# S5 exponentials and first states moved from the vector engine to Pool, the direct kernels' product interleaved over two array tiles, and a higher priority for the transposed retention outputs

## The chip, the core and the metric

One core of one Trainium2 chip runs the whole program. The metric is the device time of one execution in microseconds (us), less being better; the time before is a median of three runs. The engines are PE (matrix products), DVE (vector engine), ACT (scalar engine), POOL, and SP, which here only starts DMAs.

## What is computed

One layer of a hybrid decoder on 320 rows (256 prompt positions and 8 samples of 8 positions), all in float32. A norm and one projection give the S5 input u and, for 8 heads, q, k, v and a gate g. The S5 part needs parameters of its own, worked out on the chip from 64 groups of 64 states; the retention heads run beside it.

```python
h = rms_norm(x, norm_mix);  u, q, k, v, g = split(h @ w_in)
dt = exp(log_step);  lam_bar = exp(lam * dt)              # complex: exp(re) and cos, sin
b_bar = ((lam_bar - 1) / lam) * b
x_t = lam_bar * x_(t-1) + b_bar u_t;  y = Re(C x) + d * u # per group; samples start at x0
o = retention(rotary(q), rotary(k), v);  o = group_norm(o) * gn_w * silu(g)
x = x + concat(s5_out, o) @ w_out
x = x + (silu(h2 @ w_gate) * (h2 @ w_up)) @ w_ffn_out;  y = rms_norm(x)
```

## The kernel before

Nearly all of PE's work is the large products. Each weight is split into a high and a low part in a reduced format (`hi` by ACT on line 130, `lo` by DVE on line 131), and a block of 128 by 128 weights then takes three products of 320 columns (lines 141 to 143). `wload` fetches eight blocks at a time with three buffers each; `gemm` sums 16 blocks into one of two PSUM buffers ("acc").

The first 39 us are the prologue: 16 blocks of x are split (`xhi`, `xlo`, lines 266 to 273) beside the first weights (lines 858 and 859), and four projections run together (line 868). Then follow the projections of head 0, and for each head q, k, v, a gate and one u block (lines 905 to 918). PE and POOL keep the order in which the program emits instructions (`manual_schedule`, line 835). A small clock of estimated PE time (`clk`) and a heap of generators (`spawn`, `run_due`) decide where, between the products of a projection, the small work of a head or of an S5 chunk is emitted. DVE, ACT and SP get their order from a planner, by readiness and priority; `tc.high_priority(offset=...)` moves work forward. Every engine then runs its own queue in order.

The S5 parameters: `vexp` (line 341) evaluates an exponential by a polynomial on tiles of 128 by 32 elements. It is called for dt (line 365, `s5_step`) and for `rr`, the size of lam_bar (line 409). `s5_params` computes cos and sin by polynomials (ang, lines 370 to 405), has POOL build the rotations (`s5_turns`, line 462), forms `lp` and `gp` (powers of lam_bar and the input factors) and `lx0`, the first states of the samples (line 453: six operations on 128 by 256 elements). All small scratch tiles are cut from one tile `scrt` by `newscr` and `T`.

Chunk c of the S5 part (`s5_chunk`, from line 551) is due at 53.6 + 33.4 c on that clock. It forms `bl` and `cl`, transposes `bl` (`pt`), and runs two small products: `pb`, and `pk_` (lines 612 to 618), the direct kernels. The latter has 64 output rows per group u, so two groups lie side by side in the array (`tile_position=(0, 64 * u)`); all of u = 0 is emitted before u = 1. `lx0` is read in `s5_scan` (line 534).

A head's small work: `head_k` transposes k (`pst`) and forms the scores `pss`; `head_v` transposes v, forms `po`, the norm statistics (DVE, lines 720 to 723) and the reciprocal root (POOL, lines 726 to 733), normalises on ACT (`on`, line 736), transposes back (`pn`, line 747), and scales the result by the norm weight and the gate into `retp` (line 759, on DVE where the gate exists). `pst`, `pss`, `psr`, `pn`, `pt` and `pk_` share two PSUM buffers ("misc").

Of the kernel before, what the change touches and what calls it, by code (L numbers as in the profile page):

```python
# [44 lines left out]
def hybrid_kernel(ctx, tc, xT, w_in, w_in4, w_out, w_glu, w_fi, w_fo, vecs, s5p, bc, x0,  # L45
# [9 lines left out]
    def f(t):  # L55
        return t.bitcast(F32)
# [13 lines left out]
    o = 0  # L70
# [97 lines left out]
    def ts(out, a, s1, o1, s2=None, o2=None):  # L168
        if o2 is None:
            dve.tensor_scalar(out, a, s1, None, o1)  # L170
        else:
            dve.tensor_scalar(out, a, s1, s2, o1, o2)
        return out
# [159 lines left out]
    def T(shape):  # L333
        n = int(np.prod(shape[1:]))
        a = scr[0][:, scr[1]:scr[1] + n]
        scr[1] += n
        if len(shape) == 3:
            a = a.rearrange("p (a b) -> p a b", b=shape[2])
        return a

    def vexp(out, x, shape):
        xc = ts(T(shape), x, -87.0, ALU.max, 88.0, ALU.min)
        n = ts(T(shape), xc, 1.4426950408889634, MUL, MAGIC, ADD)
        n = ts(n, n, MAGIC, SUB)
        r = stt(T(shape), n, -LN2_PARTS[0], xc, MUL, ADD)
        r = stt(r, n, -LN2_PARTS[1], r, MUL, ADD)
        q = T(shape)
        ts(q, r, 1.0 / 5040, MUL, 1.0 / 720, ADD)
        for cf in (1 / 120, 1 / 24, 1 / 6, 0.5, 1.0, 1.0):
            tt(q, q, r, MUL)  # L350
            ts(q, q, cf, ADD)
        ni = T(shape).bitcast(I32)
        ts(n, n, 127.0, ADD)
        dve.tensor_copy(ni, n)
        ts(ni, ni, 23, ALU.logical_shift_left)
        tt(out, q, ni.bitcast(F32), MUL)

    sh = [P, NPAIR]
    she = [P, 3, NPAIR]
    shx = [P, NPAIR, NB]  # L360

    def s5_step():
        newscr(0)
        dt_ = T(sh)
        vexp(dt_, prm[:, 2], sh)
        return dt_

    def s5_params(dt_):

        ang = T(she)  # L370
        tt(ang[:, 0], prm[:, 1], dt_, MUL)
        ts(ang[:, 1], ang[:, 0], 8.0, MUL)
        ts(ang[:, 2], ang[:, 0], 64.0, MUL)
        nn = ts(T(she), ang, float(1 / np.pi), MUL, MAGIC, ADD)
        ts(nn, nn, MAGIC, SUB)
        for part in PI_PARTS:
            stt(ang, nn, -part, ang, MUL, ADD)
        par = ts(T(she), nn, 0.5, MUL, MAGIC, ADD)
        ts(par, par, MAGIC, SUB)
        stt(par, nn, 0.5, par, MUL, SUB)  # L380
        tt(par, par, par, MUL)
        ts(par, par, -8.0, MUL, 1.0, ADD)
        a2 = tt(T(she), ang, ang, MUL)
        ec, es = ecs[:, 0:NE], ecs[:, NE:]
        q = T(she)
        ts(q, a2, 1.0 / factorial(13), MUL, -1.0 / factorial(11), ADD)
        for kk in (9, 7, 5, 3, 1):
            tt(q, q, a2, MUL)
            ts(q, q, (1.0 if (kk // 2) % 2 == 0 else -1.0) / factorial(kk), ADD)
        tt(q, q, ang, MUL)  # L390
        tt(es[:, 0::3], q, par, MUL)
        q = T(she)
        ts(q, a2, -1.0 / factorial(14), MUL, 1.0 / factorial(12), ADD)
        for kk in (10, 8, 6, 4, 2, 0):
            tt(q, q, a2, MUL)
            ts(q, q, (1.0 if (kk // 2) % 2 == 0 else -1.0) / factorial(kk), ADD)
        tt(ec[:, 0::3], q, par, MUL)
        for l in range(2):
            n = (NE - 1 - l + 2) // 3
            c_, s_ = ec[:, l::3][:, :n], es[:, l::3][:, :n]  # L400
            u1, u2 = T([P, n, NPAIR]), T([P, n, NPAIR])
            tt(u1, c_, c_, MUL)
            tt(u2, s_, s_, MUL)
            tt(ec[:, l + 1::3][:, :n], u1, u2, SUB)
            stt(es[:, l + 1::3][:, :n], c_, 2.0, s_, MUL, MUL)
        s5_turns(ec, es)
        newscr(1)
        lr = tt(T(sh), prm[:, 0], dt_, MUL)
        vexp(rr, lr, sh)
        tt(lp[:, 0, 0], rr, ec[:, 0], MUL)  # L410
        tt(lp[:, 1, 0], rr, es[:, 0], MUL)
        den = tt(T(sh), prm[:, 0], prm[:, 0], MUL)
        d2 = tt(T(sh), prm[:, 1], prm[:, 1], MUL)
        tt(den, den, d2, ADD)
        rden = T(sh)
        dve.reciprocal(rden, den)
        nr = ts(T(sh), lp[:, 0, 0], -1.0, ADD)
        t1 = tt(T(sh), nr, prm[:, 0], MUL)
        t2 = tt(T(sh), lp[:, 1, 0], prm[:, 1], MUL)
        tt(t1, t1, t2, ADD)  # L420
        tt(ff[:, 0], t1, rden, MUL)
        t3 = tt(T(sh), lp[:, 1, 0], prm[:, 0], MUL)
        t4 = tt(T(sh), nr, prm[:, 1], MUL)
        tt(t3, t3, t4, SUB)
        tt(ff[:, 1], t3, rden, MUL)
        r2 = tt(T(sh), rr, rr, MUL)
        tt(r4, r2, r2, MUL)

        def cmul(o, a, b, shape):

            u1, u2 = T(shape), T(shape)
            tt(u1, a[0], b[0], MUL)
            tt(u2, a[1], b[1], MUL)
            tt(o[0], u1, u2, SUB)
            tt(u1, a[0], b[1], MUL)
            tt(u2, a[1], b[0], MUL)
            tt(o[1], u1, u2, ADD)

        def ri(t, i):
            return (t[:, 0, i], t[:, 1, i])  # L440

        def rep_(t, n):
            return tuple(t[:, q].unsqueeze(1).to_broadcast([P, n, NPAIR]) for q in range(2))

        cmul(ri(lp, 1), ri(lp, 0), ri(lp, 0), sh)
        cmul(ri(lp, slice(2, 4)), rep_(lp[:, :, 1], 2), ri(lp, slice(0, 2)), [P, 2, NPAIR])
        cmul(ri(gp, slice(0, 3)), rep_(ff, 3), ri(lp, slice(0, 3)), [P, 3, NPAIR])
        newscr(0)

        def b8(a):  # L450
            return a.unsqueeze(2).to_broadcast(shx)

        cmul((lx0[:, 0], lx0[:, 1]), (x0t[:, 0], x0t[:, 1]), (b8(lp[:, 0, 3]), b8(lp[:, 1, 3])), shx)
        for q in range(2):
            for d in range(2):
                o = lpc[:, :, q, 4 * d:4 * d + 4]
                act.mul(o, lp[:, q].rearrange("p e (c j) -> p c j e", j=4), -1.0 if d > q else 1.0)
                o = gpc[:, :, q, 4 * d:4 * d + 4]
                act.copy(o[:, :, :, 0], ff[:, q].rearrange("p (c j) -> p c j", j=4))
                act.copy(o[:, :, :, 1:], gp[:, q].rearrange("p e (c j) -> p c j e", j=4))  # L460
# [90 lines left out]
    def s5_chunk(c):  # L551
# [58 lines left out]
                    mm(0.04, pb[gs, u, NC * i:NC * i + NC], bst[us, i, gs], kst[us, 2 * (i % 2) + g],  # L610
                       start=True, stop=True, tile_position=(64 * u, 64 * g))
        pk_ = misc("pk_")
        for u in range(2):
            for i in range(2):
                for q in range(2):
                    mm(0.04, pk_[64 * u:64 * u + 64, 32 * i:32 * i + 32],
                       bl[:, q, i, u].rearrange("p e h -> p (e h)"), cl[:, q, 2 * u + i, 0],
                       start=q == 0, stop=q == 1, tile_position=(0, 64 * u))
# [74 lines left out]
    def head_v(h, v_, qg, rt, R):  # L693
# [55 lines left out]
                  (pn[:, NP:].rearrange("p (b t) -> p b t", t=32)[:, :, 0:NS],  # L749
                   retp[:, h, NP:].rearrange("p (b t) -> p b t", t=NS), slice(NP, N)))  # L750
        sg = R.get("sgt")
        for i_, o, sl in pairs_:
            if sg is None:
                act.mul(o, i_, v("gn", h))
            else:
                g_ = sg[:, sl]
                if sl.start:
                    g_ = g_.rearrange("p (b t) -> p b t", t=NS)
                stt(o, i_, v("gn", h), g_, MUL, MUL)
        R["gn"] = True  # L760
        if sg is not None:
            R["sg"] = True
# [84 lines left out]
    for k1 in (1, *range(2, KT + 1, 2)):  # L847
        with tc.high_priority(offset=100000), tc.manual_schedule(engines={mybir.EngineType.SP}):
            if k0 % 2 == 0:
                raw, hi, lo = (wp.tile([P, 8, P], d, name=n, tag=n, bufs=3).rearrange("p (k o) m -> p k o m", o=4)  # L850
                               for n, d in (("raw", F32), ("hi", F32R), ("lo", F32R)))
            q = slice(k0 % 2, (k1 - 1) % 2 + 1)
            sp.dma_start(xrs[k0 // 4][:, k0 % 4:(k1 - 1) % 4 + 1], xT[:, k0:k1])
            sp.dma_start(raw[:, q], w_in4[:, k0:k1])
            if k1 == 6:
                sp.dma_start(prm, s5p)
            split_x(k0, k1)
            act.copy(hi[:, q], raw[:, q])
            last_lo = dve.tensor_tensor(lo[:, q], raw[:, q], f(hi[:, q]), SUB)
        if k1 == 6:  # L860
            with tc.issue_after(last_lo.ins):
                dt_ = s5_step()
        if k1 % 2 == 0:
            accq = square_x(k1 - 2, k1)
        for k in range(k0, k1):
            for w_, x_ in ((hi, xhi), (hi, xlo), (lo, xhi)):
                for i, ps in enumerate(accs):
                    pe.matmul(ps, w_[:, k % 2, i], x_[:, k], start=k == 0 and w_ is hi and x_ is xhi,
                              stop=k == KT - 1 and w_ is lo)
            clk.now += 1.6  # L870
        k0 = k1
# [3 lines left out]
        sp.dma_start(t_, s_)  # L875
    for c in range(2):
        load_bc(c)
    s5_params(dt_)
    ytok = []
    rg = rstd_bcast(s5, accq, misc, "n1", ytok=ytok)  # L880

# [371 lines left out]
```

## Time and profile before

| | us |
|---|---|
| median of 3 runs (1460.18 to 1461.57) | 1460.41 |
| the profiled execution, as a run | 1462.15 |
| its span, first to last instruction | 1460.0 |
| PE busy in the span | 1441.0 |
| DVE busy | 862.5 |
| ACT busy | 607.2 |
| POOL busy | 44.4 |

A span row gives the busy time of each engine. PE's matmuls overlap, and the profile counts a matmul as busy to its modelled end. A row of a timeline gives the start, the duration, the engine, the line, the operation, the tiles written and read, and in brackets how long the engine stood idle before it and what released it.

### The profile page before, as it was taken

How to read it: one execution, taken by the hardware profiler on the slowest of the kernel's cores; microseconds unless marked ns; L12 is line 12 of the kernel's file. 1: busy time of each engine (PE TensorE's matmuls, PEld its weight loads, DVE VectorE, ACT ScalarE, POOL GpSimd, SP SyncE). 2: the span in 40 equal slices, each digit the busy share in tenths (PEclk: the TensorE clock that was granted, in tenths of full speed). 3: DMA queues.
4: the chain of work that ended last, by engine and by line, in shares of the span. 5: the costliest groups of instructions: out<-in, count | busy, mean ns of one | idle time of the engine just before them, and what ended most of it. 6: DMA issues, size and time to landing. Idle time of an engine off the chain costs nothing.

```text
span 1460.0 us, 26293 instructions
## 1 busy us (share of the span) xinstructions
PE 1441.0 (99%) x10654; PEld 1425.4 (98%) x10654; DVE 862.5 (59%) x1453; ACT 607.2 (42%) x973; POOL 44.4 (3%) x110
## 2 busy tenths in 40 slices
PE   8999999999999999999999999999999999999997
PEld 8989999999999999999999999999999999999996
DVE  8988787777656756665444444444444444444454
ACT  6455555554345533333333333333333333333452
POOL 2300000000000000000000000000000000000001
PEclk9999999999999999999999999999999999999999
DMA  7545554554644475655444445444445544444543
GB/s 259 169 150 164 157 163 151 157 154 144 224 146 146 153 246 191 213 206 174 146 157 145 126 147 175 152 152 146 131 142 165 168 145 150 145 133 146 154 145 111
DMA packets 84712, 235.38 MB, mean 161 GB/s; under 512 B 16368, under 2 KB 32368, under 8 KB 84592
## 3 DMA queue, kind: packets, MB, share of 16 engines
q1 hardware_dynamic: 83680, 231.58, 49.8%
q10 hardware_dynamic: 912, 2.14, 0.5%
q8 instruction: 84, 1.38, 0.4%
q14 instruction: 36, 0.29, 0.1%
HBM read 222.63 MB, written 8.95 MB: 159 GB/s over the span
## 4 chain that ended last, share of the span: by engine, by line
PE 70%; DVE 0%; ACT 0%; DVEq 0%; issue 0%
PE ps_fg L141 7%; PE ps_fo L141 7%; PE ps_fu L143 7%; PE ps_fg L143 7%; PE ps_fo L143 7%; PE ps_fu L141 7%; PE ps_fu L142 7%; PE ps_fg L142 7%; PE ps_fo L142 7%; PE ps_o L141 1%; PE ps_o L142 1%; PE ps_o L143 1%; PE ps_g L142 1%; PE ps_g L143 1%; PE ps_g L141 1%; DVE x L176 0%
## 5 line engine op out<-in xcount | busy, mean ns | idle before, releaser
L131 DVE TENSOR_TENSOR lo<-raw,hi 128x1024 fp32r<-128x1024 f32 (+1 forms) x416 | 467.0, 1123 | 380.9 <-ACT hi L130 380.4
L130 ACT CAST hi<-raw 128x1024 fp32r<-128x1024 f32 (+1 forms) x416 | 402.0, 967 | 680.7 <-PE ps_fo L142 188.1
L141 PE MATMUL ps_fg<-hhi,hi 128*128 128x320 f32 x704 | 217.6, 309 | 0.0
L141 PE MATMUL ps_fo<-ahi,hi 128*128 128x320 f32 x704 | 217.6, 309 | 0.0
L143 PE MATMUL ps_fo<-ahi,lo 128*128 128x320 f32 x704 | 217.6, 309 | 0.0
L142 PE MATMUL ps_fo<-alo,hi 128*128 128x320 f32 x704 | 217.6, 309 | 0.0
L141 PE MATMUL ps_fu<-hhi,hi 128*128 128x320 f32 x704 | 217.4, 309 | 0.0
L142 PE MATMUL ps_fu<-hlo,hi 128*128 128x320 f32 x704 | 217.4, 309 | 0.0
L143 PE MATMUL ps_fu<-hhi,lo 128*128 128x320 f32 x704 | 217.4, 309 | 0.0
L143 PE MATMUL ps_fg<-hhi,lo 128*128 128x320 f32 x704 | 217.4, 309 | 0.0
L142 PE MATMUL ps_fg<-hlo,hi 128*128 128x320 f32 x704 | 217.4, 309 | 0.0
L141 PE MATMUL ps_p<-xhi,hi 128*128 128x320 f32 x560 | 178.0, 318 | 0.6 <-DVE q__1093 L176 0.5
L143 PE MATMUL ps_p<-xhi,lo 128*128 128x320 f32 x560 | 173.6, 310 | 0.7 <-DVE lo L131 0.7
L142 PE MATMUL ps_p<-xlo,hi 128*128 128x320 f32 x560 | 173.2, 309 | 0.0
L142 PEld LDWEIGHTS ps_fg<-hlo,hi 128*128 128x128 f32 x704 | 132.4, 188 | 0.3
L141 PEld LDWEIGHTS ps_fg<-hhi,hi 128*128 128x128 f32 x704 | 132.4, 188 | 0.3
L141 PEld LDWEIGHTS ps_fu<-hhi,hi 128*128 128x128 f32 x704 | 132.4, 188 | 0.0
L143 PEld LDWEIGHTS ps_fu<-hhi,lo 128*128 128x128 f32 x704 | 132.4, 188 | 0.0
L142 PEld LDWEIGHTS ps_fu<-hlo,hi 128*128 128x128 f32 x704 | 132.4, 188 | 0.0
L143 PEld LDWEIGHTS ps_fg<-hhi,lo 128*128 128x128 f32 x704 | 132.4, 188 | 0.0
L141 PEld LDWEIGHTS ps_fo<-ahi,hi 128*128 128x128 f32 x704 | 132.1, 188 | 0.0
L142 PEld LDWEIGHTS ps_fo<-alo,hi 128*128 128x128 f32 x704 | 132.1, 188 | 0.0
(409 smaller groups left out, 1928.6 us busy)
## 6 DMA issues: line engine op xcount, KB each, us to landing
raw<-w_fi SPq DMA_DIRECT2D x176, 512.0 KB, 3.7
raw<-w_in SPq DMA_DIRECT2D x79, 512.0 KB, 4.0
raw<-w_fo SPq DMA_DIRECT2D x64, 512.0 KB, 3.5
raw<-w_out SPq DMA_DIRECT2D x32, 512.0 KB, 3.6
raw<-w_fo SPq DMA_DIRECT2D x64, 192.0 KB, 2.4
rt<-r SPq DMA_DIRECT2D x8, 512.0 KB, 5.4
raw<-w_glu SPq DMA_DIRECT2D x8, 512.0 KB, 3.5
raw<-r SPq DMA_DIRECT2D x8, 512.0 KB, 4.2
```

Of the source, the lines that this page charges most:

```text
L130: act.copy(hi[:, :m], raw[:, :m])
L131: dve.tensor_tensor(lo[:, :m], raw[:, :m], f(hi[:, :m]), SUB)
L141: pe.matmul(ps, hi, xhi[:, k], start=k == 0, stop=False)
L142: pe.matmul(ps, hi, xlo[:, k], start=False, stop=False)
L143: pe.matmul(ps, lo, xhi[:, k], start=False, stop=k == nk - 1)
```

## The change

Four edits. `vexp` runs on POOL (23 operations instead of 22, since POOL's form has no fused multiply and add of two tiles, and the shift is a multiplication) and is called for dt and for `rr` in a new `s5_exps`, which also forms `lr`; its POOL instructions are emitted in the prologue, where `s5_step` stood. `s5_params` takes dt and `rr` from there. The first states become a generator that emits its six operations on POOL at 54.6 of the emission clock. In the direct kernels' product the loops are turned, so that u changes fastest. The scaling of the transposed outputs (`pairs_`) is given the priority offset EVAC = 1500, as the other evacuations have.

```diff
     def vexp(out, x, shape):
-        xc = ts(T(shape), x, -87.0, ALU.max, 88.0, ALU.min)
...
+        xc = pts(T(shape), x, -87.0, ALU.max, 88.0, ALU.min)
+        n = pts(T(shape), xc, 1.4426950408889634, MUL, MAGIC, ADD)
+        pts(n, n, MAGIC, SUB)
+        r, q = T(shape), T(shape)
+        for part in LN2_PARTS:
+            pts(q, n, -part, MUL)
+            ptt(r, q, xc if part == LN2_PARTS[0] else r, ADD)
+        pts(q, r, 1.0 / 5040, MUL, 1.0 / 720, ADD)
         for cf in (1 / 120, 1 / 24, 1 / 6, 0.5, 1.0, 1.0):
+            ptt(q, q, r, MUL)
+            pts(q, q, cf, ADD)
...
+        pts(n, n, 127.0, ADD, float(2 ** 23), MUL)
+        pool.tensor_copy(ni, n)
+        ptt(out, q, ni.bitcast(F32), MUL)
...
-    def s5_step():
+    def s5_exps():
+
+        newscr(1)
+        dt_, lr = T(sh), T(sh)
+        vexp(dt_, prm[:, 2], sh)
+        pool.tensor_tensor(lr, prm[:, 0], dt_, MUL)
+        vexp(rr, lr, sh)
+        return dt_, scr[1]
...
-        lr = tt(T(sh), prm[:, 0], dt_, MUL)
-        vexp(rr, lr, sh)
...
-        cmul((lx0[:, 0], lx0[:, 1]), (x0t[:, 0], x0t[:, 1]), (b8(lp[:, 0, 3]), b8(lp[:, 1, 3])), shx)
+        def first_states():
+
+            yield max(0.0, T0 + 1.0 - clk.now)
+            newscr(0)
+            cmul((lx0[:, 0], lx0[:, 1]), (x0t[:, 0], x0t[:, 1]), (b8(lp[:, 0, 3]), b8(lp[:, 1, 3])), shx,
+                 pool.tensor_tensor)
+
+        spawn(first_states())
...
-        for u in range(2):
-            for i in range(2):
-                for q in range(2):
+        for i in range(2):
+            for q in range(2):
+                for u in range(2):
                     mm(0.04, pk_[64 * u:64 * u + 64, 32 * i:32 * i + 32],
...
+        with tc.high_priority(offset=EVAC):
+            for i_, o, sl in pairs_:
...
         if k1 == 6:
-            with tc.issue_after(last_lo.ins):
-                dt_ = s5_step()
+            exps = s5_exps()
```

## Rows read from the trace of the kernel before

**Rows 1.** The page's first part: busy time of each engine, share, instructions
```profile
PE 1441.0 (99%) x10654; PEld 1425.4 (98%) x10654; DVE 862.5 (59%) x1453; ACT 607.2 (42%) x973; POOL 44.4 (3%) x110
```
**Rows 2.** Stretches: length, then busy time of PE, PEld, DVE, ACT, POOL; granted clock
```profile
60.00:100.00 40.00, 36.74 (x285) 34.39 (x283) 35.37 (x102) 17.81 (x39) 12.51 (x25) 0.96 0.46 144
95.00:100.00 5.00, 5.00 (x60) 4.52 (x60) 3.12 (x7) 2.60 (x6) 0.00 (x0) 0.66 0.70 230
100.00:1440.00 1340.00, 1339.53 (x9970) 1328.82 (x9969) 766.79 (x1181) 548.94 (x861) 19.48 (x56) 1.00 0.50 159
```
**Rows 3.** Timeline of PE, 78 to 96 us: start, duration, line, operation, idle before
```profile
78.61 0.41 PE L143 MATMUL ps_p<-xhi,lo 128*128 128x320 f32 x1 [0.70 <-DVE lo L131]
...
81.64 0.31 PE L142 MATMUL ps_p<-xlo,hi 128*128 128x320 f32 x1
81.79 0.31 PE L143 MATMUL ps_p<-xhi,lo 128*128 128x320 f32 x1
82.60 0.42 PE L141 MATMUL ps_p<-xhi,hi 128*128 128x320 f32 x1 [0.50 <-DVE q__1093 L176]
...
95.00 1.38 PE L102 MATMUL pss<-q__1093,k__1169 128*128 128x256 f32 x6 [1.93 <-DVE retp L180]
```
**Rows 4.** Timeline of DVE: the two scalings of head 0's transposed outputs
```profile
87.01 0.48 DVE L180 SCALAR_TENSOR_TENSOR retp<-pn,vec,sg 128x256 f32<-128x256 f32 x1
...
94.67 0.28 DVE L180 SCALAR_TENSOR_TENSOR retp<-pn,vec,sg 128x64 f32<-128x64 f32 x1
```
**Rows 5.** Stretch of the second exponential, instructions on the scratch tile: length, DVE busy
```profile
58.90:67.80 8.90, 6.17 (x19) 1.00 0.36 121
```
**Rows 6.** Tile scrt: first four of the six operations of the first states
```profile
L176 DVE TENSOR_TENSOR scrt<-x0t,lp x4: 417/418/421, 74.2 to 79.6; 128x256 f32<-128x256 f32 x4
```
**Rows 7.** Timeline of all engines, 63 to 66 us: DVE and POOL side by side
```profile
63.15 1.72 DVE L131 TENSOR_TENSOR lo<-raw,hi 128x1024 fp32r<-128x1024 f32 x1
63.86 1.60 POOL L479 TENSOR_TENSOR e<-e,ta 128x256 f32<-128x256 f32 x1
64.79 0.71 DVE L170 TENSOR_SCALAR scrt<-scrt 128x32 f32<-128x32 f32 x1
```
**Rows 8.** Timeline of POOL: an operation on 32 elements
```profile
68.31 0.27 POOL L488 TENSOR_TENSOR tabl<-tabl,ta 128x32 f32<-128x32 f32 x1
```
**Rows 9.** Timelines of DVE and PE in the prologue: low weights formed, and first used
```profile
15.33 1.16 DVE L859 TENSOR_TENSOR lo<-raw,hi 128x1024 fp32r<-128x1024 f32 x1
...
19.04 0.31 PE L868 MATMUL py<-xhi,lo 128*128 128x320 f32 x1
```
**Rows 10.** Tile prm, the input of the exponentials: DMA issue (last: start) and landing
```profile
L856 SPq DMA_DIRECT2D prm<-s5p x1: 701/701/701, 4.6 to 4.6; - x1
...
DMA to landing us min/median/max: 6.5/6.5/6.5
```
**Rows 11.** Timelines of DVE and POOL at the start
```profile
3.42 4.73 DVE L170 TENSOR_SCALAR xhi<-u,vec 128x320 fp32r<-128x320 f32 x1 [3.42 <-DMA vec<-vecs]
...
7.74 0.24 POOL L464 MEMSET e<- 128x64 f32 x1
```
**Rows 12.** Direct kernels, chunk 1: timeline, tile view, and its matmuls in two stretches
```profile
131.13 0.91 PE L102 MATMUL pk__1760<-cl,bl 128*64 128x32 f32 x16
131.97 0.42 PE L141 MATMUL ps_p<-xhi,hi 128*128 128x320 f32 x1
...
L102 PE MATMUL pk__1760<-cl,bl x16: 222/223/243, 131.1 to 131.8; 128*64 128x32 f32 x16
...
131.12:131.38 0.26, 0.25 (x4) 1.00 0.36 125
131.38:131.58 0.20, 0.20 (x10) 1.00 0.12 26
```
**Rows 13.** Timelines of DVE and PE: the first norm's root, and its first reader
```profile
43.52 0.15 DVE L180 SCALAR_TENSOR_TENSOR ry<-rt,ry 128x3 f32<-128x3 f32 x1
...
45.81 0.49 PE L102 MATMUL ps_r<-ident,ry 128*128 128x128 f32 x3
```

More of the change, by code (lines that the diff above doesn't have):

```diff
@@ L341, in vexp, with pts @@
     def vexp(out, x, shape):
-        xc = ts(T(shape), x, -87.0, ALU.max, 88.0, ALU.min)
[L343 to L348, printed above, removed]
+        def pts(out, a, s1, o1, s2=None, o2=None):
+            if o2 is None:
+                pool.tensor_scalar(out, a, s1, None, o1)
+            else:
+                pool.tensor_scalar(out, a, s1, s2, o1, o2)
+            return out
+        ptt = pool.tensor_tensor
+        xc = pts(T(shape), x, -87.0, ALU.max, 88.0, ALU.min)
[6 more added lines that the diff above has]
+        pts(q, r, 1.0 / 5040, MUL, 1.0 / 720, ADD)
         for cf in (1 / 120, 1 / 24, 1 / 6, 0.5, 1.0, 1.0):
-            tt(q, q, r, MUL)
-            ts(q, q, cf, ADD)
+            ptt(q, q, r, MUL)
+            pts(q, q, cf, ADD)
         ni = T(shape).bitcast(I32)
[L353 to L356, printed above, removed]
+        pts(n, n, 127.0, ADD, float(2 ** 23), MUL)
+        pool.tensor_copy(ni, n)
+        ptt(out, q, ni.bitcast(F32), MUL)
     sh = [P, NPAIR]
@@ L360, in hybrid_kernel, with s5_params @@
     shx = [P, NPAIR, NB]
-    def s5_step():
+    def s5_exps():
[5 more added lines that the diff above has]
+        return dt_, scr[1]
+    def s5_params(dt_, used):
         newscr(0)
[L364 to L368, printed above, removed]
         ang = T(she)
@@ L407, in s5_params @@
         newscr(1)
-        lr = tt(T(sh), prm[:, 0], dt_, MUL)
-        vexp(rr, lr, sh)
+        scr[1] = used
         tt(lp[:, 0, 0], rr, ec[:, 0], MUL)
@@ L427, in s5_params, with cmul @@
         tt(r4, r2, r2, MUL)
-        def cmul(o, a, b, shape):
+        def cmul(o, a, b, shape, tt=tt):
             u1, u2 = T(shape), T(shape)
@@ L447, in s5_params @@
         cmul(ri(gp, slice(0, 3)), rep_(ff, 3), ri(lp, slice(0, 3)), [P, 3, NPAIR])
-        newscr(0)
         def b8(a):
             return a.unsqueeze(2).to_broadcast(shx)
-        cmul((lx0[:, 0], lx0[:, 1]), (x0t[:, 0], x0t[:, 1]), (b8(lp[:, 0, 3]), b8(lp[:, 1, 3])), shx)
+        def first_states():
[4 more added lines that the diff above has]
+        spawn(first_states())
         for q in range(2):
@@ L751, in head_v @@
         sg = R.get("sgt")
[L752 to L759, printed above, removed]
+        with tc.high_priority(offset=EVAC):
+            for i_, o, sl in pairs_:
+                if sg is None:
+                    act.mul(o, i_, v("gn", h))
+                else:
+                    g_ = sg[:, sl]
+                    if sl.start:
+                        g_ = g_.rearrange("p (b t) -> p b t", t=NS)
+                    stt(o, i_, v("gn", h), g_, MUL, MUL)
         R["gn"] = True
@@ L858, in hybrid_kernel @@
             act.copy(hi[:, q], raw[:, q])
-            last_lo = dve.tensor_tensor(lo[:, q], raw[:, q], f(hi[:, q]), SUB)
+            dve.tensor_tensor(lo[:, q], raw[:, q], f(hi[:, q]), SUB)
         if k1 == 6:
-            with tc.issue_after(last_lo.ins):
-                dt_ = s5_step()
+            exps = s5_exps()
         if k1 % 2 == 0:
@@ L877, in hybrid_kernel @@
         load_bc(c)
-    s5_params(dt_)
+    s5_params(*exps)
     ytok = []
```

## The prediction

> **What bounds the kernel now.** I read the page's busy times first, then the busy time of PE by stretches, then the timelines where PE stands idle. PE is busy 1441.0 of 1460.0 us [rows 1]. From 100 to 1440 us it is busy 1339.53 of 1340 at full clock, although DVE and ACT are used there for about half of the time [rows 2]. So the PE stream sets the time, and an edit counts only if it shortens that stream or removes a wait in it. Freeing another engine gives nothing by itself.
>
> Waits that can be removed lie between 60 and 100 us: PE is busy 36.74 of 40 there while DVE is busy 35.37, and the granted clock is 0.96 [rows 2]. Three waits carry most of the 3.26 us, and DVE ends each of them [rows 3]: 0.70 for `lo` weights, 0.50 for the rotary of head 1's q (the PSUM buffer was not free), 1.93 before head 1's scores `pss`. The last is a matter of buffers. `pss` needs the misc buffer that holds head 0's transposed outputs `pn`. Their first part is scaled at 87.01 and the second at 94.67, ending at 94.95 [rows 4]; `pss` starts at 95.00. After this longest wait the clock falls: over 95 to 100 us it is granted at 0.66 on average [rows 2], a mixture of the 2.4 and the 1.2 GHz level.
>
> **The change part by part.**
>
> *Priority for the transposed outputs.* Both scalings move ahead of unhurried work in DVE's queue. They cost what they did (0.48 and 0.28 [rows 4]) and only change place. Behind them queue `lo` and the S5 chunk's work, later by 0.76 us at most; three weight buffers cover that. If DVE reached them before `pn` is written it would wait with all of its queue, but it is behind schedule there. So the 1.93 us go. The idle is counted from a modelled end: matmuls start 0.15 apart but are 0.31 long, so each wait hides 0.16 more (81.79 to 82.60 is 0.81, of which 0.15 is the pace and 0.50 is shown [rows 3]). Worth 1.93 + 0.16 = 2.1 us, with ends 0 (another buffer or DVE itself is late next) and 2.1. The low clock goes with the wait: 5.0 us at 0.66 did the work of 3.3, so 1.7 us, with ends 0 and 1.7, since it hangs on that wait.
>
> *The second exponential leaves DVE.* Between 58.9 and 67.8 us its instructions take 6.17 us of DVE [rows 5]. They are this long because POOL builds the rotations at the same time and the two engines hold each other up. A 32-element operation takes 0.71 us and ends at 65.50, just after POOL's operation of 63.86 ends at 65.46; and that POOL operation outlasted DVE's `lo`, which ends at 64.87 [rows 7]. With these and the first states gone, `lp`, `gp`, head 0's statistics and the evacuations come earlier, and the other two waits should go: 0.70 + 0.50 + 2 x 0.16 = 1.5 us, with ends 0 and 1.5. Small waits make up the rest of the 3.26, 0.1 us.
>
> The Trainium skill (SBUF — State Buffer, section "SBUF: two separate sides") says that the port pair which DVE and GpSimd share is an exclusive lock held for a whole instruction. Rows 7 agree.
>
> *The first states leave DVE.* Six operations of 0.418 are 2.5 us of DVE [rows 6]. On POOL they are 256-element operations between 0.64 (the part of the row at 63.86 that lies after DVE's `lo` is 0.59) and 1.60 [rows 7]: 3.5 to 9.6 us. POOL starts them after head 0's root, and their first reader is chunk 0's scan, far behind the waits above. They hold DVE up about as much as they free it. Cost and gain nothing; if DVE lost all 9.6 us, that would be the first rival.
>
> *Both exponentials enter POOL in the prologue.* prm lands at 4.6 + 6.5 = 11.1 us [rows 10]. Two times 23 operations and one for `lr` are 47, at 0.27 each [rows 8] 12.7 us if nothing is in the way; as DVE is nearly full there, about one goes in behind each DVE operation, so I estimate that dt is ready near 25 and `rr` near 40 us. DVE loses the first exponential's 22 small operations. Each POOL operation may hold up one DVE operation by 0.27. The slack: `lo` weights are formed at 15.33 + 1.16 = 16.49 and first used at 19.04, so 2.55 us [rows 9]. About ten DVE operations from 11.1 to there could lose 2.7, just over it: 0 to 0.15 us on PE. The norm's root ends at 43.67 and PE reads it at 45.81, a slack of 2.1 [rows 13]; its chain of 11 tiny operations could lose 3.0 if `rr` is still being computed: 0 to 0.9 us. A gain is excluded, since PE doesn't wait at either place. I take 0.3, nearer to nothing because the first exponential frees DVE there; ends 0 and 1.1. DVE also gets a new wait: its angle work now waits for dt from POOL, and everything queued behind it (the splits of weights) waits too.
>
> *POOL's queue at the start.* Two memsets for the rotations now stand behind the exponentials. Before, the first `xhi` on DVE took 4.73 us, until 8.15, because POOL's memsets ran until 7.98 [rows 11]. It should end about 0.25 us earlier and PE's first product with it. Ends 0 and 0.3; I take 0.2.
>
> *Direct kernels.* The 8 products appear as 16 matmuls, from 131.13 to the next product at 131.97: 0.84 us [rows 12]. In the first 0.26 us four start, all of u = 0, one each 0.065 us. In the next 0.20 us ten are in flight; three of them are old ones (each lasts 0.223), so seven start, 0.029 each: here the two array tiles run beside each other. With u changing fastest they do so from the beginning, and u = 1 starts about 0.25 us earlier. Eight chunks: 8 x 0.25 = 2.0 us. Ends 1.0 and 2.1: at least half of the head start should go, and more than 0.26 isn't there. Nothing waits on the order, since each u has its own output rows.
>
> The Trainium skill (TensorE: Matmul & The Clock Gate, section "Part 3: Packing small matmuls — row/col tiling") says that matmuls start strictly in program order. Rows 12 differ: seven starts in 0.20 us can't be one tile's. By that rule each u would be held behind the other's second matmul, and the part would save an estimated 8 x 0.19 = 1.5 us.
>
> **The sum.** 2.1 + 1.7 + 1.5 + 0.1 - 0.3 + 0.2 + 2.0 = 7.3 us. The profiled execution took 1462.15 us (span 1460.0 and 2.15 around it), 1.7 above the median; nothing before the first or after the last instruction changes, so it would become 1454.8. From the median: 1460.41 - 7.3 = **1453.1 us**.
>
> **The rivals.**
>
> *The relief is only moved.* POOL's operations hold up DVE as much as they free it. The waits of 0.70 and 0.50 stay (+1.5 us), the prologue costs its full 1.1 (+0.8), and DVE's wait for dt may bring one stall with a fallen clock (+1.7): 1454.6 to 1457.1. For it: rows 7. Against it: the exponentials go to a time at which POOL is idle, out of a stretch where it is busy for 12.51 us [rows 2].
>
> The Trainium skill (Perfetto Trace Analysis, section "Optimizing Scalar/DVE Operations") warns that moving work between GPSIMD and DVE might not help, because of the shared port. That rule is this rival.
>
> *The priority doesn't bring what it says.* DVE's order is planned anew, and a misc buffer is late at another place by about the same 2.1 us, with its 1.7 us of clock: 1453.1 + 3.8 = 1456.9. For it: the planner sets the order from its own durations, and with two buffers one late reader is enough. Against it: later heads, with the old priority, show no such wait [rows 2].
>
> *POOL starves DVE: slower.* Place: the prologue from 11.1 us. The memsets kept one DVE operation waiting for over 4 us [rows 11]. If the 47 operations leave DVE as little room, it loses 12.7 us; less the slack of 2.55, PE loses 10.1, and one fall of the clock 1.7: 1453.1 + 11.8 = 1464.9. It decides from a loss of about 10 us. Against it: the memsets don't depend on each other, while each step of a polynomial needs the one before, and between 58.9 and 67.8 DVE got its operations through between POOL's [rows 5, 7].
>
> **How the numbers follow.** Forecast 0.60, relief only moved 0.18, priority without effect 0.14, starved 0.08. The likeliest gives 1453.1. Its own range is 1450.5 to 1456. The low end of the whole takes every end above (2.1 + 1.7 + 1.5 + 0.1 + 0.3 + 2.1 = 7.8 us gives 1452.6) and up to 1.5 us for restarts after waits and smaller delays that the rows don't show, with the runs' own spread: 1450. The high end takes in both rivals that stay faster or the same, with that spread: 1459. A difference below 0.2%, 2.9 us, can't be told from no change. The forecast and most of the first two rivals are faster: 0.60 + 0.13 + 0.08 = 0.81; the same: 0.12; slower: 0.07.
>
> **What would show it.** Right: no wait of `pss` for `retp` near 93 us and a granted clock of 1.00 from 60 to 100; PE busy over 39 of 40 us there; the 16 matmuls of the direct kernels in about 0.59 us; `xhi` ended before 8.0; POOL's exponentials done before 45. Wrong: a PE wait in the prologue, an operation of POOL released by DVE or the reverse for over 1 us, a new wait for a misc buffer, or DVE idle behind `dt`.

## The result, and the profile after

The changed kernel takes 1465.12 us (median of 6 runs, 1463.93 to 1466.92), beside 1460.53 for the kernel before in the same runs: 1.0033 times as long, with a 95% interval of 1.0020 to 1.0046. It is slower by 4.6 us; 1453.1 had been forecast. Its profiled execution took 1465.23 us, with a span of 1463.2 (before 1460.0).

First the page's busy line, and PE's waits up to 100 us (what waited, for whom: total, times, longest).

```profile
PE 1437.4 (98%) x10654; PEld 1422.6 (97%) x10654; DVE 854.0 (58%) x1402; ACT 607.7 (42%) x973; POOL 74.3 (5%) x163
```
```profile
PE pst L107 <- ACT kv L697: 5.3, 1, 5.3
PE ps_r L102 <- DVE u L176: 3.6, 1, 3.6
PE py L886 <- ACT hi L877: 2.5, 3, 1.9
PE ps_p L141 <- DVE k__776 L176: 2.0, 1, 2.0
```

POOL does 29.9 us more than before and DVE 8.5 less [rows 1], as meant. But the second exponential and the first states alone took about 6.2 and 2.5 us of DVE [rows 5, 6], and the first exponential left it too: what stayed on DVE has become longer. The waits of before for `retp`, `lo` and q [rows 3] are gone. Three others stand in their place: 3.6 us for the sums of squares (`u`), 2.0 for the rotary of k, and 5.3 for `kv`, the copies of the transposed k. The waits for `hi` belong to the start, of which more below.

Stretches (columns as in [rows 2]: length, then PE, PEld, DVE, ACT, POOL busy; granted clock). First one of the kernel before that [rows 2] doesn't have, then the kernel after:

```profile
20.00:40.00 20.00, 20.00 (x139) 20.00 (x138) 18.14 (x41) 12.52 (x23) 0.00 (x0) 1.00 0.76 235
```
```profile
20.00:40.00 20.00, 16.97 (x116) 16.71 (x114) 12.52 (x19) 9.69 (x17) 16.39 (x38) 1.00 0.61 198
41.00:45.00 4.00, 4.00 (x19) 4.00 (x20) 3.96 (x20) 2.99 (x7) 0.00 (x0) 0.57 0.51 156
68.40:72.00 3.60, 3.60 (x15) 3.60 (x16) 2.31 (x10) 2.67 (x8) 1.83 (x7) 0.50 0.00 0
60.00:100.00 40.00, 34.68 (x243) 34.15 (x242) 32.23 (x74) 17.90 (x39) 19.24 (x34) 0.91 0.50 147
95.00:100.00 5.00, 5.00 (x37) 5.00 (x36) 1.66 (x2) 2.37 (x3) 0.00 (x0) 1.00 0.91 266
100.00:1440.00 1340.00, 1339.53 (x10021) 1328.45 (x10020) 768.11 (x1184) 550.12 (x865) 19.97 (x56) 1.00 0.50 159
```

PE loses 3.03 us between 20 and 40 us, where it lost nothing before, and from 60 to 100 it is busy 34.68 of 40, against 36.74 before [rows 2]. From 100 us on nothing is lost, before or after [rows 2]. From 95 to 100 us the clock is back at 2.4 GHz, as forecast. But it falls to 1.2 GHz behind each of the two long new waits: to 0.57 of full speed on average from 41 to 45 us and to 0.50 from 68.4 to 72.

Where the time went is seen by following the same four products in both traces. First the kernel before (the fourth block's first product, the sums of squares, the transpose of v, chunk 0's direct kernels), then the kernel after:

```profile
16.10 0.31 PE L868 MATMUL py<-xhi,hi 128*128 128x320 f32 x1
39.87 0.72 PE L102 MATMUL ps_r<-ones,u 128*128 128x1 f32 x6
58.62 0.55 PE L107 MATMUL pst<-ident,v__784 128*128 128x128 f32 x3 [0.27 <-ACT kv L679]
99.21 0.91 PE L102 MATMUL pk__1318<-cl,bl 128*64 128x32 f32 x16
```
```profile
13.05 0.31 PE L886 MATMUL py<-xhi,hi 128*128 128x320 f32 x1
40.60 0.83 PE L102 MATMUL ps_r<-ones,u 128*128 128x1 f32 x6 [3.62 <-DVE u L176]
68.33 0.90 PE L107 MATMUL pst<-ident,v__780 128*128 128x128 f32 x3 [5.32 <-ACT kv L697]
104.28 0.66 PE L102 MATMUL pk__1320<-cl,bl 128*64 128x32 f32 x16
104.87 0.41 PE L141 MATMUL ps_p<-xhi,hi 128*128 128x320 f32 x1
```

After minus before, the kernel after stands at -3.05, +0.73, +9.71, +5.07 us, and at the end of the span at +3.2. So it starts 3 us ahead, for a reason of its own (below). It loses 3.78 up to the sums of squares: the 3.62 of the wait and the 0.16 that each wait hides. It loses 9.0 more up to the transpose of v: 1.7 for the low clock (4.0 us at 0.57 do the work of 2.3), 2.2 for k, and 5.1 for `kv` (5.32 less the 0.27 of before). Then it wins 4.6 back by chunk 0, where the old waits and the old fall of the clock are missing; these come to 3.6 and 1.7, less 1.8 for the new low clock from 68.4 to 72, or 3.5, and where the other 1.1 come from is open. It wins 1.9 in the last stretch, the direct kernels of all eight chunks: their 16 products take 0.59 us now (104.28 to 104.87), against 0.84 [rows 12].

**The first new wait.** DVE in the kernel after, from 30.8 us, and POOL's last operation on `rr`:

```profile
30.83 0.82 DVE L176 TENSOR_TENSOR u<-u,retp 128x640 f32<-128x640 f32 x1
31.58 0.19 DVE L176 TENSOR_TENSOR scrt<-prm,scrt 128x32 f32<-128x32 f32 x1
39.05 0.19 DVE L176 TENSOR_TENSOR scrt<-rr 128x32 f32<-128x32 f32 x1 [7.28 <-POOL rr L365]
39.16 0.82 DVE L176 TENSOR_TENSOR u<-u,retp 128x640 f32<-128x640 f32 x1
40.06 0.48 DVE L176 TENSOR_TENSOR u<-u 128x320 f32<-128x320 f32 x1
```
```profile
38.76 0.25 POOL L365 TENSOR_TENSOR rr<-scrt 128x32 f32<-128x32 f32 x1
```

The row at 39.05 is `r2 = rr * rr`, the first of the two squarings that give `r4` (lines 438 and 439 of the kernel after). In the order that the planner made, it stands ahead of the last two additions of the sums of squares. `rr` comes from POOL at 39.01. In the kernel before, DVE forms `rr` itself, and the first squaring follows half a microsecond later:

```profile
67.15 0.61 DVE L176 TENSOR_TENSOR rr<-scrt 128x32 f32<-128x32 f32 x1
...
68.20 0.18 DVE L176 TENSOR_TENSOR scrt<-rr 128x32 f32<-128x32 f32 x1
```

So DVE in the kernel after stands idle for 7.28 us before an operation of 0.19, with additions behind it that need nothing from POOL; and PE waits for them.

**The second.** ACT in the kernel after, from 64 us:

```profile
64.39 0.37 ACT L477 COPY gpc<-ff 128x32 f32<-128x32 f32 x2 [3.47 <-DVE ff L176]
64.94 0.37 ACT L477 COPY gpc<-ff 128x32 f32<-128x32 f32 x2 [0.19 <-DVE ff L176]
65.19 0.62 ACT L696 ACTIVATE kd<-pst,kdc 128x128 f32<-128x128 f32 x2
67.16 0.74 ACT L475 ACTIVATE lpc<-lp 128x128 f32<-128x128 f32 x2 [1.36 <-DVE lp L176]
67.91 0.36 ACT L697 ACTIVATE kv<-pst,kdc 64x128 f32<-64x128 f32 x1
```

The copies of the S5 tables (`gpc`, `lpc`) wait for DVE's `ff` and `lp`, which are worked out from `rr` and from the cosines and sines. In the new order they stand ahead of `kd` and `kv`, which empty the buffer of the transposed k, for which PE waits. In the kernel before, `kv` ends at 58.57 and the first `gpc` follows at 70.51:

```profile
58.21 0.36 ACT L679 ACTIVATE kv<-pst,kdc 64x128 f32<-64x128 f32 x1
...
70.51 0.37 ACT L459 COPY gpc<-ff 128x32 f32<-128x32 f32 x2 [3.67 <-DVE ff L176]
```

Theory A was therefore: the change moves the producer of `rr` to a slower engine, the planner, which orders DVE and ACT, moves the readers of `rr` forward, and DVE and ACT, each working through its queue in order, hold urgent work behind them. The rival B: POOL's small operations slow DVE itself (the forecast's last rival, whose 1464.9 us is nearly the measured time). The profile already speaks against B: in the prologue DVE's `lo` of 1024 elements takes 1.16 to 1.32 us beside POOL's operations, and 1.16 to 1.23 before. A second question was whether the exponentials on POOL pay once nothing waits for them wrongly.

### The profile page after: what moved, and what is told of

The parts are those of the page before. It is cut to its first block, busy times and chain, and to the rows that moved or that the text cites. A ratio compares the mean times of both kernels' runs of the same rounds, so it can differ in the third digit from the quotient of the medians.

```text
span 1463.2 us, 26296 instructions
## 1 busy us (share of the span) xinstructions
PE 1437.4 (98%) x10654; PEld 1422.6 (97%) x10654; DVE 854.0 (58%) x1402; ACT 607.7 (42%) x973; POOL 74.3 (5%) x163
## 4 chain that ended last, share of the span: by engine, by line
PE 70%; DVE 0%; ACT 0%; DVEq 0%; issue 0%
PE ps_fg L141 7%; PE ps_fo L143 7%; PE ps_fo L142 7%; PE ps_fu L143 7%; PE ps_fg L143 7%; PE ps_fu L142 7%; PE ps_fg L142 7%; PE ps_fu L141 7%; PE ps_fo L141 7%; PE ps_o L143 1%; PE ps_o L141 1%; PE ps_o L142 1%; PE ps_g L142 1%; PE ps_g L143 1%; PE ps_g L141 1%; DVE x L176 0%
```

## The experiments

Ratios are to the kernel before on the same chip, with 95% intervals. Across chips they compare better than medians: the kernel before itself has medians from 1459.51 to 1462.20. Two ratios that differ by less than about 0.0018 (2.6 us) can't be told apart.

| kernel | median | ratio to before |
|---|---|---|
| the change | 1465.12 | 1.0033 (1.0020 to 1.0046) |
| e1 loop order alone | 1458.42 | 0.9990 (0.9981 to 1.0000) |
| e2 priority alone | 1456.34 | 0.9976 (0.9966 to 0.9985) |
| e3 move to POOL alone | 1467.87 | 1.0051 (1.0039 to 1.0064) |
| e4 change, squarings on POOL | 1462.34 | 1.0013 (1.0004 to 1.0021) |
| e5 change, squarings later | 1458.09 | 0.9983 (0.9974 to 0.9993) |
| e6 change, kd and kv first | 1461.61 | 1.0006 (0.9997 to 1.0015) |
| e7 both | 1456.24 | 0.9966 (0.9953 to 0.9980) |
| e8 loop order and priority | 1456.21 | 0.9966 (0.9953 to 0.9979) |
| e9 e8, first scaling on ACT | 1454.63 | 0.9957 (0.9944 to 0.9969) |
| e10 change, `rr` on DVE | 1456.84 | 0.9973 (0.9961 to 0.9984) |
| e11 e8, first states on POOL | 1457.37 | 0.9974 (0.9964 to 0.9984) |
| e12 e10, first scaling on ACT | 1454.96 | 0.9961 (0.9948 to 0.9973) |
| e13 e5, table copies behind kv | 1457.11 | 0.9964 (0.9951 to 0.9977) |
| e14 e13, first scaling on ACT | 1455.24 | 0.9954 (0.9942 to 0.9966) |
| e15 before, first scaling on ACT | 1459.24 | 0.9982 (0.9973 to 0.9990) |

### The parts, each alone

e1, the kernel before with the loops of the direct kernels turned:

```diff
-        for u in range(2):
-            for i in range(2):
-                for q in range(2):
+        for i in range(2):
+            for q in range(2):
+                for u in range(2):
                     mm(0.04, pk_[64 * u:64 * u + 64, 32 * i:32 * i + 32],
```

> The kernel before with the loops of the direct kernels' product turned and nothing else. Array tiles run beside each other from the start: the 16 matmuls of a chunk go from 0.84 us to about 0.59, eight chunks, so 2.0 us faster than before (about 1458.5). Starts strictly in order: 1.5 us faster. No effect of the order: the same time as before. None of these expects a change in the waits between 60 and 100 us, since DVE's queue is not touched.

Measured 1458.42 against 1459.51, 1.1 us less, with an interval from 0 to 2.8. In its trace the 16 products take 0.59 us, as in the kernel after. The runs alone can't tell 1.1 from 2.0; the rows give 8 times 0.25.

e2, the kernel before with the priority:

```diff
-        for i_, o, sl in pairs_:
+        with tc.high_priority(offset=EVAC):
+            for i_, o, sl in pairs_:
...
```

> The kernel before with the priority of the two scalings and nothing else. If the edit does what was predicted, the wait of 1.93 us for the second scaling goes and the clock with it: 3.8 us faster than before (about 1456.7). If DVE is merely late as a whole between 60 and 100 us, the wait moves to the next reader of a buffer: within 1 us of before.

Measured 1456.34, 3.2 us less. PE's wait for `retp` is gone from the trace; those for `lo` (0.7) and q (0.5) stay. A wait of 1.3 us for the rotary of k is there, which the profiled execution of the kernel before doesn't have; more on it under "The start".

e3, the move to POOL alone (the changed kernel with the two diffs above taken back):

> Exponentials and first states on POOL, without the other two edits. Theory A (a DVE operation queued early waits in order for rr from POOL, and the norm's sums behind it): the wait of PE for the sums of squares near 37 us and the two later waits stay as in the changed kernel; the time is that of the changed kernel plus the 2 us of the direct kernels, 1467, or less if the priority edit has a share in the later waits. Rival B (the loss comes from the priority edit reordering DVE and ACT): faster than before by 1 to 2 us.

Measured 1467.87, 8.4 us more than before. PE waits 3.8 us for `u` and 4.8 for `kv`, the pair of the full change. With e1 and e2, 8.4 - 1.1 - 3.2 = 4.1 us; the change measured 4.6. The parts add within the intervals, and the whole loss is in the move to POOL.

### Which wait of the move

e4, the changed kernel with the two squarings on POOL, where they stand in `s5_params`:

```diff
-        r2 = tt(T(sh), rr, rr, MUL)
-        tt(r4, r2, r2, MUL)
+        r2 = T(sh)
+        pool.tensor_tensor(r2, rr, rr, MUL)
+        pool.tensor_tensor(r4, r2, r2, MUL)
```

> The changed kernel, but the two squarings that read rr first (r2, r4) are on POOL behind the exponentials, so nothing on DVE reads rr before the cosines are there. Theory A: DVE's wait of 7.28 us at 31.6 us goes, the wait of PE for the sums of squares (3.6 us) and its 1.7 us of low clock go; 1465.1 falls to 1459 at least, and to 1451 if the later waits of PE (2.0 for k, 5.3 for the transposes of v, 1.7 of clock) came from the same lateness. Rival C (POOL and DVE hold each other up at the port): DVE stays late by as much, PE still waits over 2 us before 45 us, and the time stays above 1463.

Measured 1462.34, over the 1459 that theory A allowed. The wait for the sums of squares is gone, but PE's waits and ACT's queue show where it went:

```profile
PE pst L107 <- ACT kv L698: 7.6, 1, 7.6
```
```profile
62.17 0.61 ACT L591 COPY d<-r 128x504 f32<-128x504 f32 x1 [8.69 <-POOL r L440]
64.05 0.61 ACT L697 ACTIVATE kd<-pst,kdc 128x128 f32<-128x128 f32 x2
```

In POOL's program order the squarings stand behind the rotations, so `r4` comes at 62.1. ACT's copy of it (`d`) stands ahead of `kd`. The wait changed its engine, from DVE to ACT, and the same PE stands behind it. So its time can't tell the two theories apart; e5's can.

e5, the changed kernel with the squarings on DVE, behind the last step of the norm's root:

```diff
...
-            rsqrt(ms, y, tmp)
+            last_ry = rsqrt(ms, y, tmp)
+        if ytok is not None:
+            with tc.issue_after(last_ry.ins):
+                tt(r4, rr, rr, MUL)
+                tt(r4, r4, r4, MUL)
...
-        r2 = tt(T(sh), rr, rr, MUL)
-        tt(r4, r2, r2, MUL)
...
```

> The changed kernel with one move: the two squarings that give the fourth power of the decay stay on DVE, but behind the last step of the norm's root (and so behind the sums of squares), not ahead of them. Nothing else differs by hand. Theory A (DVE, working in order, waits for POOL's second exponential at 31.8 to 39.1 us and holds the last sums of squares): PE's wait for the sums of squares (3.6 us) and the one for k (2.0 us) are gone and the clock stays at 2.4 GHz from 40 to 60, so at least 5 us less than the changed kernel: 1456 to 1460; if the lp chain comes earlier by as much, the 5.3 us wait for kv shrinks with it, down to 1452. Rival B (POOL's small operations slow DVE itself by their port, wherever they are awaited): DVE is as late as before, 1463 to 1465.

Measured 1458.09, and PE's waits up to 100 us are:

```profile
PE pst L107 <- ACT kv L699: 4.9, 1, 4.9
...
PE ps_p L141 <- DVE k__776 L176: 0.7, 1, 0.7
```

The last addition of the squares starts at 31.37 us instead of 40.06, and the wait for it is gone. The ratio is 0.0050 under that of the change, or 7.3 us: theory A. The 47 POOL operations of the exponentials stand where they stood, and PE is busy for all of the 20 us from 20 to 40. Rival B, which expected 1463 to 1465, is out. The wait for `kv` hardly changes (4.9), and 0.7 of the wait for k stays.

e6, the changed kernel with priority for `kd` and `kv`:

```diff
+        with tc.high_priority(offset=EVAC):
             for i in range(2):
                 act.mul(kd[:, i], pst[:, P * i:P * i + P], kdc[:, h, i:i + 1])
             act.mul(kv[64:128, h], pst[64:128, 2 * P:3 * P], kdc[64:128, h, 2:3])
```

> The changed kernel with priority 1500 for ACT's three copies of the transposed k (kd twice and kv), so that they stand ahead of the copies of the S5 tables (lpc and the second gpc pair) in ACT's queue. Theory A2 (the 5.3 us wait of PE for kv is ACT waiting in order for DVE's lp and ff): the wait falls to under 2.5 us (the first gpc pair still stands ahead and waits for ff), the clock's fall near 68 to 72 us is shorter, and the time is 3 to 6 us under the changed kernel: 1459 to 1462; the first wait (ps_r, 3.6 us) stays. Rival (kv is late because DVE and PE are late ahead of it): the wait stays over 4 us, 1464 to 1466.

Measured 1461.61, 0.0027 or 3.9 us under the change. The wait for `kv` falls from 5.3 to 2.7 us; the first pair of table copies still stands ahead. The wait for the sums of squares stays, at 3.9.

e7, both edits:

> Both moves together: the squarings behind the root, and the priority for kd and kv. If the two waits are separate, the savings add: 8 to 13 us under the changed kernel, 1452 to 1457, about what the forecast was (1453). If the second wait is a consequence of the first, this is the same as the kernel with the squarings moved alone, within 1.5 us.

Measured 1456.24, 0.0067 or 9.8 us under the change; the two alone give 11.2. So they are two causes, independent as far as the intervals tell. 2.7 us of the wait for `kv` stay here too.

### Does the move to POOL pay when nothing waits wrongly?

e8, the kernel before with loop order and priority, and no move:

> The kernel before with the order of the direct kernels' loop and the priority, without the move to POOL. If the parts add: 1460.5 less 3.2 (priority alone) less 1.1 (loop order alone) = 1456, between 1455 and 1457, under both kernels. If the move to POOL were needed for the priority to pay (rival: the wait that the priority takes away would have come back elsewhere), over 1458.

Measured 1456.21: the same as e7, on the same chip, and under both kernels of the case. The 9.8 us that the two edits win back only pay for the move.

e10, only dt's exponential and the first states on POOL:

```diff
...
-        pool.tensor_tensor(lr, prm[:, 0], dt_, MUL)
-        vexp(rr, lr, sh)
...
+        lr = tt(T(sh), prm[:, 0], dt_, MUL)
+        vexp_dve(rr, lr, sh)
...
```

Here `vexp_dve` is the form of the kernel before.

> The changed kernel with only the first exponential (that of the time step) on POOL; the second (that of the decay) is back on DVE, the first states stay on POOL. Theory A (the harm is that the decay comes from POOL later than DVE's and ACT's queues are ordered for): no wait of PE for the sums of squares, kd and kv stand ahead of the table copies again, the wait for kv is under 1 us: 1454 to 1457. Rival (POOL's operations in the prologue are harmful by themselves, since the first exponential is the one that runs beside the busy DVE): 1459 or more.

Measured 1456.84. With `rr` back on DVE there is no wait for the squares, and `kv` costs 0.3 us. The first exponential is the one that runs beside a busy DVE, and it does no harm there: from 20 to 40 us PE is busy all the time. From 60 to 100 us, though, PE is busy 36.99 of 40, against 38.67 in e8; why is open.

e11, e8 with only the first states on POOL (the edit of the change):

> The kernel before with the loop order and the priority, and of the move to POOL only the first states (6 products and sums of 128 x 32 x 8). Expected: they were off PE's path on DVE, so within 1.5 us of the kernel without them (1456.2): 1454.7 to 1457.7. Rival (DVE is what sets 72 to 90 us, so 2.5 us of DVE are 2.5 us of the time): under 1454.5; or POOL is slower and chunk 0 comes later: over 1458.

Measured 1457.37; its ratio, 0.9974, is 0.0008 over that of e8, within the intervals. They cost and gain nothing that can be told by the time.

e13, e5 with all table copies behind head 0's last `kv`, so that no copy waits ahead of it:

```diff
-        for q in range(2):
-            for d in range(2):
+        def tables():
+            while "kv0" not in rot_t:
+                yield 0.3
+            with tc.issue_after(rot_t["kv0"].ins):
+                for q in range(2):
+                    for d in range(2):
...
+        spawn(tables())
...
```

> The changed kernel with the squarings behind the norm's root, and all of ACT's copies of the S5 tables (lpc, gpc) issued behind head 0's last kv copy. Both of DVE's and ACT's waits for POOL's exponentials then stand behind what PE needs. If the exponentials on POOL pay what the forecast gave them (waits of 0.7 and 0.5 us gone, 1.5 us): 1453 to 1455, with PE's wait for kv under 0.5 us, and under the kernel without the move to POOL (1456.2) by 1.5 us or more. Rival (the relief is only moved): 1455.5 to 1457.5.

Measured 1457.11, ratio 0.9964, against 0.9966 without the move (e8). PE's waits from 20 to 100 us, first in e13, where the one for `kv` is now as short as in the kernel before, then in e8:

```profile
PE po L102 <- DVE sm L176: 1.4, 1, 1.4
PE ps_p L141 <- DVE k__764 L176: 0.7, 1, 0.7
PE ps_p L141 <- DVE q__1095 L176: 0.7, 1, 0.7
PE ps_p L143 <- DVE lo L131: 0.3, 1, 0.3
PE pst L107 <- ACT kv L705: 0.3, 1, 0.3
```
```profile
PE ps_p L143 <- DVE lo L131: 0.7, 1, 0.7
PE ps_p L141 <- DVE k__780 L176: 0.6, 1, 0.6
PE ps_p L141 <- DVE q__1093 L176: 0.5, 1, 0.5
PE pst L107 <- ACT kv L679: 0.3, 1, 0.3
```

The waits that the move was to take away (`lo` 0.70, q 0.50 [rows 3]) are at 0.3 and 0.7, and a new one for the masked scores `sm` is at 1.4. Without the wait for k, which comes and goes with the start (below), the waits are 2.7 us with the move and 1.5 without. DVE and POOL in e13:

```profile
58.19 0.81 DVE L176 TENSOR_TENSOR scrt<-lp 128x64 f32<-128x64 f32 x1
59.03 0.69 DVE L176 TENSOR_TENSOR lp<-scrt 128x64 f32<-128x64 f32 x1
59.64 0.61 DVE L176 TENSOR_TENSOR sm<-pss,mk 128x256 f32<-128x256 f32 x2
```
```profile
58.18 0.73 POOL L505 TENSOR_TENSOR e<-e,ta 128x256 f32<-128x256 f32 x1
```

What runs beside POOL's rotations is now the chain of `lp`, and it has become slow instead of the exponential: its 64-element operations last about as long as POOL's beside them, 0.81 and 0.73, and `sm` queues behind. In the kernel before the same operation on `lp` took 0.22 at 73.3 us, when the rotations were over. The relief is only moved. The Trainium skill (Perfetto Trace Analysis, section "Optimizing Scalar/DVE Operations") warns that work moved between GPSIMD and DVE might not help, since they share a port. These rows agree.

### The start

In the kernel before, DVE's first scaling took 4.73 us [rows 11]; in the kernel after 1.31:

```profile
3.28 1.31 DVE L170 TENSOR_SCALAR xhi<-u,vec 128x320 fp32r<-128x320 f32 x1 [3.28 <-DMA vec<-vecs]
```

The forecast had put the 4.73 down to POOL's memsets and expected about 0.25 us less. But e8, which leaves POOL's queue as it was, shows 1.27, and e11, from the same source but for the first states, 4.73:

```profile
3.32 1.27 DVE L170 TENSOR_SCALAR xhi<-u,vec 128x320 fp32r<-128x320 f32 x1 [3.32 <-DMA vec<-vecs]
```
```profile
3.42 4.73 DVE L170 TENSOR_SCALAR xhi<-u,vec 128x320 fp32r<-128x320 f32 x1 [3.42 <-DMA vec<-vecs]
```

So the short scaling doesn't need the change. Whether the change makes it more frequent isn't shown: it is short in all eight traces with an exponential on POOL and the scaling on DVE, and in two of the five without. An early start also isn't all gain. The three traces with the long scaling have no wait for k, and 13 of the other 14 have one, of 0.2 to 2.0 us, among them e2, e8, e9 and e15, which leave the exponentials on DVE. To take DVE out of the contest, the scaling goes to ACT, which does all the others:

```diff
-            if k == 0:
-                ts(xhi[:, k], xr, v("g_mix", k), MUL)
-            else:
-                act.mul(xhi[:, k], xr, v("g_mix", k))
+            act.mul(xhi[:, k], xr, v("g_mix", k))
```

e15, with this alone in the kernel before:

> The kernel before with the first scaling on ACT and nothing else. If the start is a race that costs 3 us in a part of the runs: its runs lie within 2 us of each other, near the fastest of the kernel before (1457 to 1459, against 1460.7 median and a spread of 5.6 us). Rival (the spread comes from elsewhere): median and spread as before.

Measured 1459.24, with 11 runs from 1457.70 to 1460.03, against 1462.20 for the kernel before, with 17 runs from 1457.96 to 1463.81. The median falls by 3.0 us (by the ratio 2.6, 1.5 to 3.9) and the spread from 5.9 to 2.3. Of the 17 runs before, 14 lie at 1461.20 or above and three at 1459.48 or below. So the race between DVE's scaling and POOL's memsets is real; that the 14 are the runs with the long scaling is likely but not shown: each trace shows one run. ACT takes 0.56 us for the scaling.

e9, the same in e8:

> The kernel before with the loop order and the priority, and in addition the first input tile's scaling (xhi, k = 0) on ACT, as for all the others, not on DVE. Theory (the start is a race: DVE's first scaling runs beside POOL's memsets and takes 1.2 or 4.7 us, by chance from run to run, and PE's first product waits for it): PE's first product starts at 5.0 to 5.5 us in every run, the runs lie closer together, and the median is 1.5 to 3 us under that of the kernel without this edit: 1453 to 1455 against 1456.2. Rival (the spread comes from elsewhere, or ACT's later scaling costs the same 3 us by pushing its casts back): 1456 or more.

Measured 1454.63 (1453.78 to 1455.35). e12, the same in e10:

> The first exponential and the first states on POOL, the second exponential on DVE, the loop order, the priority, and the first scaling on ACT: the candidate for the best. If the parts add: 1.5 to 3 us under the kernel without the scaling on ACT, 1452 to 1455. If the race at the start is not the cause of the spread: the same as without it.

Measured 1454.96, on the same chip as e10's 1456.84. e14, the same in e13:

> The same with the first scaling on ACT: 1 to 2 us under it, 1452 to 1454, if both are as thought; then it would be the fastest of all. Rival: as the kernel without the move to POOL and with the scaling on ACT (1454.6).

Measured 1455.24, on the same chip as e13's 1457.11, and not under e9 as hoped. By their medians both win 1.9 us, which their intervals don't separate from nothing; e15 alone is clear. The three can't be told apart by their ratios. e9 is the simplest: two edits of the change, one of the start, nothing on POOL, 0.43% under the kernel before.

## Why the prediction was wrong

**What held.** PE's stream sets the time, and only waits in it count. The priority was worth what its rows said: 3.8 forecast, 3.2 measured alone (2.2 to 5.0), with the wait for `retp` gone and, in the kernel after, the clock whole from 95 to 100 us. The direct kernels take 0.59 us, as forecast to the hundredth, so the rows give the forecast 2.0 us. By the strict program order that the Trainium skill states (TensorE: Matmul & The Clock Gate, section "Part 3: Packing small matmuls — row/col tiling") the part was to bring an estimated 1.5 us; the runs of e1 can't tell the two apart. `rr` was put near 40 us and came at 39.01, partly by luck: dt, put near 25, came at 29.5, and the second exponential made up for it because DVE stood idle beside it. In e5, where DVE works on, `rr` comes at 41.15. DVE's angle work at 31.58 didn't have to wait for dt.

**What failed** is the step "Both exponentials enter POOL in the prologue": -0.3 us, ends 0 and 1.1. It counted what POOL's operations do to DVE beside them, and looked for DVE's new wait at the angle work, for dt alone. It had a time for `rr` (40 us) but never asked which operations read `rr`, and where in DVE's and ACT's queues they would stand: the squarings, and after them `d`, `gpc` and `lpc`. In the kernel before `rr` was formed on DVE itself at 67 us, so all of these stood late. With `rr` gone from DVE the planner put the squarings into the prologue; why it chose so is open. The step left out 3.8 + 1.7 + 2.2 + 5.1 us up to the transpose of v, and about 1.8 for the clock from 68.4 to 72 (3.6 us at 0.50): 14.6 us in the profiled execution. The 2.2 for k are the least sure of them: e3 and e6, with the same wait for `u`, wait 0.9 and 0.5 there, and e2, e8, e9 and e15, which leave the exponentials on DVE, 0.6 to 1.6. That the planner would make a new order was written in the second rival, for the misc buffer alone.

**The second step that failed** is the second exponential's 1.5 us. e7 and e13 have the exponential off DVE and the wait for `u` gone, e13 that for `kv` too, and they are no faster than e8: ratios of 0.9966 and 0.9964 against 0.9966. The times alone would still allow 1.5 us, but e13's waits don't: the 1.4 for `sm` stands where 0.4 for `lo` was won and 0.2 for q lost. The relief was moved, by the forecast's own first rival, which had 0.18.

**The rivals.** "POOL starves DVE" gave 1464.9 and the measurement is 1465.1, but its mechanism is not what happened: in e5, e7 and e13 POOL runs the same operations at the same place, and PE is busy for all of the 20 us from 20 to 40. DVE was not starved; it stood idle for 7.28 us. That the two times nearly agree is luck.

**The start** has a hand in the comparison of the two profiled executions: the kernel after began 3.05 us ahead by the race. The forecast's sign for it, `xhi` ended before 8.0, was met (4.59), but not for its reason, the two memsets that stand later: that was luck. How much of the lead is left at the end isn't shown: at the sums of squares the kernel after stood 0.73 us behind, the lead having gone into the wait for `u`. The spans differ by 3.2 us, the medians, each over six runs, by 4.6.

The first wait, for `u`, is shown by e5, and the second, for `kv`, by e6, e7 and e13: each goes or shrinks when the reader ahead of it is put behind. What makes the first scaling fall to one side or the other at the start stays open.

## What to carry to other kernels

When a value's producer moves to another engine, list every reader of it, the cheap ones above all, with the engine and the place in its queue, and set the measured time of the producer against what stands behind the reader: an operation of 0.19 us held DVE for 7.28. Where a planner makes the order, pin such readers behind the urgent work by hand. And freeing an engine that doesn't set the time pays nothing by itself: with both waits mended the move to POOL was worth nothing that the runs can tell, while a priority on two operations was worth 3.2 us.

## What the runs showed of the hardware

The same instruction, DVE's scaling of 128 by 320 elements beside POOL's memsets, takes 1.2 to 1.3 us or 4.7 to 4.8, with nothing between in any of these traces; it starts at 3.28 to 3.39 us in the first case and at 3.38 to 3.42 in the second, so the start doesn't decide it alone. In the ten short cases it ends at 4.58 to 4.61 us whatever its start, 0.2 us after POOL's memset `kbd`, and POOL's last large memsets (`cl`) begin at 5.64 or 5.65. In the three long ones it ends at 8.15, 0.17 us after POOL's last memset, and `cl` begins at 5.45. This reads as one gap between POOL's memsets: either DVE gets in there and POOL loses 0.2 us, or DVE waits for all that follow. Why it misses the gap isn't shown.

POOL's operations on 32 elements depend on how busy DVE is. In the kernel after the 23 of the first exponential, beside a busy DVE, went from 12.35 to 29.50 us, 0.75 us each. The 23 of the second, most of them while DVE stood idle, went from 29.91 to 39.01, 0.40 each. The forecast's estimate of 0.27 [rows 8] holds for neither: with DVE idle one operation takes 0.21 to 0.30, but the starts of two dependent ones lie 0.29 to 0.39 apart.
